# Three depthwise-conv tiles as half-length filters that are summed by accumulating transfers

## The chip, the cores and the metric

The kernel runs on one core of a Trainium2 chip, in one launch. The time is device microseconds for the whole program, median of 3 runs. TensorE is called PE here, VectorE DVE, ScalarE ACT, GpSimd POOL and SyncE SP, as in the profile. All data is float32. A matmul of float32 operands is done as three matmuls in a shorter format: each operand is split into a rounded part (`hi`) and the remainder (`lo`), and hi*hi, hi*lo and lo*hi are summed in PSUM. So every weight tile and every activation tile needs a cast (on ACT) and a subtraction that gives the remainder.

## What is computed

One layer over 1024 tokens and 1024 channels:

```python
h = rmsnorm(x, norm_g) * (1 + scale(c)) + shift(c)
cv, cg, cs, lx, ls = split(h @ w_in)              # 5 x 1024 columns
v = cv * sigmoid(cg)
v = causal_depthwise_conv(v, dw_w, dw_b)          # 31 taps for each channel
v = silu(layernorm(v, cln_g, cln_b))              # over channels
y_conv = (v @ pw2_w + pw2_b) * silu(cs)
xs = causal_depthwise_conv(lx, sc_w, sc_b)        # 4 taps
r, i = sigmoid(xs @ wr + br), sigmoid(xs @ wi + bi)   # 8 blocks of 128
y_lru = linear_scan(a(r), bx(r, i, xs)) * silu(ls)
x = rmsnorm(x + (1 + gate(c)) * (concat(y_conv, y_lru) @ w_out), final_g)
```

## The kernel before, in words

Channels lie on the 128 partitions, tokens along the free dimension, so an activation is eight tiles of 128 x 1024 float32 (512 KB). A weight tile of 128 output channels is also 128 x 1024. PE works through slots: a slot is one output tile, 8 contraction steps x 3 products x 2 halves of the tokens, 48 matmuls of 128 x 512 (`mm_k`, L432 to 450). The slots' order stands in `slots` (L377 to 392): first the tiles for conv tiles 0 and 1, then the tiles of the recurrence, mixed with those for conv tiles 2 to 7; then eight slots (`lru`) that multiply the recurrence's output with its half of `w_out`. After the layer norm of the conv result come the pointwise projection (`papw`, `pbpw`) and the rest of `w_out` (`paout`, `pbout`, `out`).

Each engine works in order through its own queue. The order is not written by hand: `Plan` (L83 to 245) takes every operation with an engine, a cost, a priority and what it reads and writes, plays the kernel through with these costs, and emits the operations in the order in which they started there. What the chip then does later than the plan, the queues' order doesn't follow. The plan holds DVE operations with operands in SBUF and POOL operations apart from each other (`lock`). Tiles come from pools: 47 tiles of 128 x 1024 in SBUF (`big`), in PSUM three tiles of 128 x 1024 for matmuls (`mm`) and one for accumulation (`acc`).

What the change touches:

- `weights` and `w_slice` (L410 to 430): load a weight tile (SP), cast to `whi` (ACT), remainder `wlo` by a subtraction `SUB` (L323), on POOL except for the four `out` tiles at the end.
- `gate_mod` (L1028) and `dot` (L710): eight dot products of a row of `mod_w` with the conditioning vector: on POOL a multiply, then on ACT a sum along the row; on DVE one operation.
- `gw_load` (L949): remainders of the gate weights, on POOL.
- `conv_tile` (L886 to 938): the 31 taps. For the tiles in `POOLED`, 2 and 5, ACT makes a product `cq` of the shifted tile with each tap, 30 of them at full length, and POOL adds each to the tile (`c<-c,cq`). For the other six the tokens are parted into even and odd, and three filters of half length run on DVE: one over the even tokens, one over the odd ones, one over their sums with taps summed in pairs. Each tap is one multiply-add of up to 512 elements into the accumulator `cacc` in PSUM; the two outputs are then put together. Conv work has the lowest priority (1000 and up), behind all that PE waits for.
- `conv_sum` (L940): the sum of the eight conv tiles, on POOL but for the last; `layer_norm` (L1037): the mean by PE from it, then mean, variance and their broadcast.
- `evac_in` (L961): takes a finished tile out of PSUM; the multiply that gives `v` reads pairs of tokens (`by_two`) and writes even and odd ones apart (`apart`).

Of the kernel before, what the change touches and what calls it, by code (L numbers as in the profile page):

```python
# [45 lines left out]
POOLED = (2, 5)  # L46
# [6 lines left out]
SUMS = (0, 1, 3, 2, 4, 6, 5, 7)  # L53
QRES = 4
GM = 22
# [22 lines left out]
class Op:  # L78
    __slots__ = ("eng", "cost", "emit", "prio", "table", "bufs", "succ", "wait", "ready",
                 "seq", "reserve", "columns", "lock", "end", "psum")  # L80


class Plan:  # L83
# [7 lines left out]
    def __init__(self, pools):  # L91
        self.pools = pools
        self.ops, self.writer, self.readers = [], {}, {}
# [13 lines left out]
    def op(self, eng, cost, emit, prio, r=(), w=(), table=None, after=(), reserve=0,  # L107
           columns=0, lock=False):
        o = Op()
        o.eng, o.cost, o.emit, o.prio, o.table = eng, cost, emit, prio, table  # L110
# [28 lines left out]
    def order(self):  # L139
# [19 lines left out]
        def done(o, end):  # L159
            o.end = until[o.eng] = end  # L160
# [14 lines left out]
        while left:  # L175
# [3 lines left out]
            for e in engines:  # L179
# [42 lines left out]
                if e == "POOL" and held["DVE"] > t + 1e-9:  # L222
                    waiting, until[e] = o, float("inf")
                    continue
# [24 lines left out]
def hymba_layer(ctx: ExitStack, tc: tile.TileContext, xT, c_row, vecs, mod_w, w_first, w_in,  # L249
# [11 lines left out]
    psacc = ctx.enter_context(tc.tile_pool(name="psacc", bufs=1, space=bass.MemoryType.PSUM))  # L261
# [8 lines left out]
    pools["acc"] = (psacc, "acc", [P, T], 1)  # L270
# [46 lines left out]
    def TT(prio, eng, out, a, b, op, n=T, r=(), w=(), reserve=0, after=()):  # L317
        e = dve if eng == "DVE" else pool
        return S.op(eng, d_cost(n) if eng == "DVE" else p_cost(n),
                    lambda: e.tensor_tensor(out=out(), in0=a(), in1=b(), op=op), prio, r, w,  # L320
                    reserve=reserve, lock=not in_psum(r), after=after)

# [104 lines left out]
    def weights(s, after=(), n=None, eng="POOL"):  # L427
        n = number[s] if n is None else n
        w_bufs(s)
# [25 lines left out]
    def acc_tile(name, parts=2):  # L455
        return S.buf("acc", name, F32, parts)
# [187 lines left out]
    psf = [mm_tile(f"first{n}", 4) for n in range(3)] + [acc_tile("first3", 4)]  # L644
    psb = psf[3]
# [15 lines left out]
    def fw_mm(prio, ps, i, xh, xl, k, cols, after=()):  # L661
        _, wh, wl = fw[k - k % 2]

        def emit():
            for lhs, rhs, last in ((wh, xh, 0), (wh, xl, 0), (wl, xh, 1)):
                for a, b in cols:
                    pe.matmul(ps()[:, a:b], fw_part(lhs, k, i * P, i * P + P)(),  # L667
# [92 lines left out]
    st, wk = ctile("st", KT), halves(psb, H, T)  # L760

    def stats(sq, k):
        for b in range(KT):
            pe.matmul(psb()[:, H + b:H + b + 1], sq()[:, b * P:b * P + P], ones[:, 0:1],
                      start=k == 0 and b == 0, stop=k == len(sqs) - 1, skip_group_check=True)

    def spread_mm(a, e):
        for b in range(a // P, e // P):
            o = H + b * P - a
# [4 lines left out]
    ACT(RSP, lambda: st, lambda: psb()[:, H:H + KT], AF.Sqrt, KT, bias=eps_t, scale=1.0 / D,  # L774
        r=wk, w=[("st", 0)])
    S.op("DVE", 0.12, lambda: dve.reciprocal(st, st), RSP, [("st", 0)], [("st", 0)])
    for a, e in START:
        spread = S.op("PE", 0.22 * ((e - a) // P), lambda a=a, e=e: spread_mm(a, e), RSP,
                      [("st", 0)], wk, columns=4 * (e - a))
        ACT(RSP, part(rbc, a, e), part(psb, H, H + e - a), "copy", e - a, r=wk,  # L780
# [83 lines left out]
    def by_two(b, a, e):  # L864
        return lambda: b()[:, a:e].rearrange("p (m q) -> p m q", q=2)

    def apart(b, a, e):
        return lambda: b().rearrange("p (q m) -> p m q", q=2)[:, a // 2:e // 2]
# [16 lines left out]

    def conv_tile(i):  # L886
# [6 lines left out]
        if i in POOLED:  # L893
            ACT(pr, ci, vi, AF.Identity, scale=w(0), bias=vec("dw_b", i), r=[vi, ("V", 1)],
                w=[ci])
            for s in range(1, TAPS):
                q = big_buf(f"cq{i}_{s}")
                ACT(pr, part(q, s, T), part(vi, 0, T - s), AF.Copy, T - s, scale=w(s), r=[vi],
                    w=[q], reserve=QRES)
                TT(pr, "POOL", part(ci, s, T), part(ci, s, T), part(q, s, T), ALU.add, T - s,  # L900
                   r=[ci, q], w=[ci])
            c[i] = ci
            return


        acc, b2 = acc_tile(f"cacc{i}"), bias2[:, i:i + 1]
        acc_e, acc_s, src_s = half(acc, 0), half(acc, 1), half(ci, 0)
# [8 lines left out]
        def every(o):  # L916
            return lambda: ci().rearrange("p (m q) -> p q m", q=2)[:, o]
        TT(pr, "DVE", src_s, ev, od, ALU.add, H, r=[vi], w=[(ci, 0)])
        ACT(pr, acc_e, ev, AF.Identity, H, scale=w(0), bias=vec("dw_b", i), r=[vi, ("V", 1)],
            w=[(acc, 0)])  # L920
        ACT(pr, acc_s, src_s, AF.Identity, H, scale=ws(0), bias=b2,
            r=[(ci, 0), ("V", 1), ("wsum", 0)], w=[(acc, 1)])
        for r in range(1, 16):
            STT(pr, cut(acc_e, r, H), cut(ev, 0, H - r), w(2 * r), cut(acc_e, r, H), ALU.mult,
                ALU.add, H - r, r=[vi, (acc, 0)], w=[(acc, 0)])
            STT(pr, cut(acc_s, r, H), cut(src_s, 0, H - r), ws(r), cut(acc_s, r, H), ALU.mult,
                ALU.add, H - r, r=[(ci, 0), (acc, 1)], w=[(acc, 1)])
        ACT(pr, every(1), acc_s, "copy", H, r=[(acc, 1)], w=[ci])
        ACT(pr, acc_s, od, AF.Copy, H, scale=w(1), r=[vi], w=[(acc, 1)])
        for r in range(1, 15):  # L930
            STT(pr, cut(acc_s, r, H), cut(od, 0, H - r), w(2 * r + 1), cut(acc_s, r, H), ALU.mult,
                ALU.add, H - r, r=[vi, (acc, 1)], w=[(acc, 1)])
        ACT(pr, every(0), acc_e, "copy", H, r=[(acc, 0)], w=[ci])
        TT(pr, "DVE", every(1), every(1), acc_e, ALU.subtract, H, r=[ci, (acc, 0)], w=[ci])
        TT(pr, "DVE", every(1), every(1), acc_s, ALU.subtract, H, r=[ci, (acc, 1)], w=[ci])
        TT(pr, "DVE", cut(every(0), 1, H), cut(every(0), 1, H), cut(acc_s, 0, H - 1), ALU.add,
           H - 1, r=[ci, (acc, 1)], w=[ci])
# [11 lines left out]
    def gw_load(i, n):  # L949
# [4 lines left out]
        SUB(n - 3, "POOL", lo, r, hi, 2 * P, r=[r, hi], w=[lo])  # L954
# [6 lines left out]
    def evac_in(m, ps, n, b=None, rb=()):  # L961
# [5 lines left out]
        elif kind == CV:  # L967
            sg = sig.pop(i)
            if i in POOLED:
                v[i] = sg  # L970
                TT(pr, "DVE", sg, ps, sg, ALU.mult, r=[ps, sg], w=[sg])
            else:
                v[i] = big_buf(f"v{i}")
# [331 lines left out]
```

## Time and profile before

| | |
|---|---|
| median of 3 runs | 770.2 us (769.64 to 770.25) |
| the profiled execution | 771.28 us |
| its span, first to last instruction | 769.4 us |
| mean granted TensorE clock | 0.985 of full speed |
| shares of the chain that ended last | PE 57%, DVE 29%, ACT 7%, POOL 3% |

The profile is one execution on the chip. A row of a timeline gives start and duration in us, the engine, the line of the kernel (often that of a helper: L438 is every slot's matmul, L320 every tensor_tensor, L312 every scalar_tensor_tensor, L301 and L293 ACT's operations), what is written and read, how many in a row, and in brackets the idle time ahead of it and the operation that ended it. A row of groups gives, after the bar, busy us, mean ns of one, and idle time. A row of stretches gives for each engine its busy time and in brackets the number of operations, then the granted clock, the busy share of the 16 DMA engines and GB/s. Matmuls overlap, so that one takes longer than the distance to the next.

### The profile page before, as it was taken

How to read it: one execution, taken by the hardware profiler on the slowest of the kernel's cores; microseconds unless marked ns; L12 is line 12 of the kernel's file. 1: busy time of each engine (PE TensorE's matmuls, PEld its weight loads, DVE VectorE, ACT ScalarE, POOL GpSimd, SP SyncE). 2: the span in 40 equal slices, each digit the busy share in tenths (PEclk: the TensorE clock that was granted, in tenths of full speed). 3: DMA queues.
4: the chain of work that ended last, by engine and by line, in shares of the span. 5: the costliest groups of instructions: out<-in, count | busy, mean ns of one | idle time of the engine just before them, and what ended most of it. 6: DMA issues, size and time to landing. Idle time of an engine off the chain costs nothing.

```text
span 769.4 us, 8629 instructions
## 1 busy us (share of the span) xinstructions
PE 733.5 (95%) x3288; PEld 606.0 (79%) x3288; DVE 665.6 (87%) x806; ACT 420.3 (55%) x473; POOL 323.1 (42%) x132
## 2 busy tenths in 40 slices
PE   3999899999999997999999998999999999999995
PEld 2888677888888885888888787788888888887885
DVE  7999999789899889999897998995977666999565
ACT  6630926997626477955956565664723223455220
POOL 0030312799899469989999612121220000000000
PEclk9999999999999999899999999999999999999997
DMA  9930221102102312331111012433332621425114
GB/s 329 406 118 32 83 82 35 55 27 83 63 28 83 116 55 83 116 110 56 55 55 55 27 55 81 138 136 111 136 115 96 200 110 40 152 83 177 43 55 164
DMA packets 24954, 77.84 MB, mean 101 GB/s; under 512 B 2768, under 2 KB 6096, under 8 KB 24912
## 3 DMA queue, kind: packets, MB, share of 16 engines
q1 hardware_dynamic: 24912, 77.28, 28.5%
q8 instruction: 26, 0.43, 0.2%
q14 instruction: 16, 0.13, 0.1%
HBM read 64.68 MB, written 12.58 MB: 100 GB/s over the span
## 4 chain that ended last, share of the span: by engine, by line
PE 57%; DVE 29%; ACT 7%; POOL 3%; issue 2%; DMA 1%; SPq 0%; DVEq 0%; ACTq 0%; POOLq 0%
PE ps L438 32%; DVE cacc L312 11%; PE first L667 6%; PE papw L559 5%; PE pbpw L559 4%; PE out L605 3%; ACT cq L301 3%; PE paout L559 2%; DVE r L1020 2%; PE pbout L559 2%; DVE xs L312 1%; DVE xs L320 1%; DVE yl L320 1%; DVE sls L320 1%; POOL c L320 1%
## 5 line engine op out<-in xcount | busy, mean ns | idle before, releaser
L320 POOL TENSOR_TENSOR wlo<-raw,whi 128x1024 fp32r<-128x1024 f32 x44 | 115.1, 2615 | 234.5 <-ACT whi L293 234.5
L438 PE MATMUL ps<-uh,whi 128*128 128x512 f32 x576 | 180.5, 395 | 7.0 <-ACT scs L301 6.6
L438 PE MATMUL ps<-ul,whi 128*128 128x512 f32 x576 | 179.7, 393 | 3.6 <-DVE ul L312 3.6
L438 PE MATMUL ps<-uh,wlo 128*128 128x512 f32 x576 | 179.3, 393 | 1.6 <-POOL wlo L320 1.6
L320 POOL TENSOR_TENSOR c<-c,cq 128x1023 f32<-128x1023 f32 (+29 forms) x60 | 159.8, 2663 | 9.5 <-ACT cq L301 7.0
L312 DVE SCALAR_TENSOR_TENSOR cacc<-v,V,cacc 128x511 f32<-128x511 f32 (+14 forms) x174 | 129.6, 745 | 13.7 <-ACT c L293 6.3
L438 PEld LDWEIGHTS ps<-uh,whi 128*128 128x128 f32 x576 | 109.4, 191 | 31.4 <-ACT scs L301 7.5
L438 PEld LDWEIGHTS ps<-ul,whi 128*128 128x128 f32 x576 | 109.3, 190 | 27.7 <-DVE ul L312 4.7
L438 PEld LDWEIGHTS ps<-uh,wlo 128*128 128x128 f32 x576 | 109.2, 190 | 24.8 <-POOL wlo L320 2.0
L293 ACT CAST whi<-raw 128x1024 fp32r<-128x1024 f32 x48 | 50.3, 1047 | 59.6 <-issue 34.4
L301 ACT ACTIVATE cq<-sig,V 128x1023 f32<-128x1023 f32 (+29 forms) x60 | 63.9, 1128 | 1.6 <-POOL c L320 1.6
L312 DVE SCALAR_TENSOR_TENSOR cacc<-c,wsum,cacc 128x511 f32<-128x511 f32 (+6 forms) x84 | 62.7, 746 | 2.3
L301 ACT ACT_TABLE_LOAD x45 | 57.7, 1283 | 1.6 <-PEq L1297 0.7
L438 PE MATMUL ps<-yh,whi 128*128 128x512 f32 x128 | 39.6, 391 | 0.0
L438 PE MATMUL ps<-yh,wlo 128*128 128x512 f32 x128 | 39.4, 389 | 0.0
L438 PE MATMUL ps<-yl,whi 128*128 128x512 f32 x128 | 39.4, 389 | 0.0
L667 PE MATMUL first<-uh,fhi 128*128 128x512 f32 x64 | 26.7, 416 | 11.1 <-ACT uh L301 11.1
L312 DVE SCALAR_TENSOR_TENSOR xs<-ps,V,xs 128x1023 f32<-128x1023 f32 (+2 forms) x24 | 30.6, 1274 | 2.6 <-ACT xs L301 2.5
L438 PEld LDWEIGHTS ps<-yl,whi 128*128 128x128 f32 x128 | 24.0, 188 | 5.0
L438 PEld LDWEIGHTS ps<-yh,wlo 128*128 128x128 f32 x128 | 24.0, 188 | 5.0
L667 PE MATMUL first<-ul,fhi 128*128 128x512 f32 x64 | 26.3, 411 | 1.7 <-DVE ul L312 1.7
L438 PEld LDWEIGHTS ps<-yh,whi 128*128 128x128 f32 x128 | 23.9, 188 | 4.9
(299 smaller groups left out, 1359.7 us busy)
## 6 DMA issues: line engine op xcount, KB each, us to landing
raw<-in_w_in_dram SPq DMA_DIRECT2D x36, 512.0 KB, 3.3
modw<-in_mod_w_dram SPq DMA_DIRECT2D x24, 512.0 KB, 7.8
raw<-in_w_out_dram SPq DMA_DIRECT2D x12, 512.0 KB, 3.9
scsd<-scs SPq DMA_DIRECT2D x8, 512.0 KB, 2.6
acc<-in_xT_dram SPq DMA_DIRECT2D x8, 512.0 KB, 4.6
accd<-acc SPq DMA_DIRECT2D x8, 512.0 KB, 2.8
rawpw<-in_pw_dram SPq DMA_DIRECT2D x8, 512.0 KB, 3.8
scsr<-scsd SPq DMA_DIRECT2D x8, 512.0 KB, 5.3
```

Source lines behind the costliest of these rows:

```text
L293: act.copy(out(), in_())
L301: act.activation(out=out(), in_=in_(), func=func, **kw)
L312: dve.scalar_tensor_tensor(out=out(), in0=in0(), scalar=scalar, in1=in1(), op0=op0, op1=op1, accum_out=accum)
L320: lambda: e.tensor_tensor(out=out(), in0=a(), in1=b(), op=op), prio, r, w,
L438: pe.matmul(ps()[:, a - off:b - off], k3(lhs)()[:, k, :], rhs[k]()[:, a:b], start=(k == 0 and lhs is wh and rhs is xh and (a - off) % H == 0),
L559: pe.matmul(half(*ps)(), half(*lhs)()[:, j * P:j * P + P], half(*rhs)(), start=start and j == 0 and z == 0, stop=j == KT // 2 - 1 and z == ...
L605: pe.matmul(ps()[:, a - off:e - off], k3(lhs)()[:, k, :], rhs()[:, i * H + a % H:i * H + a % H + e - a], start=k == KORD[0] and lhs is wh ...
L667: pe.matmul(ps()[:, a:b], fw_part(lhs, k, i * P, i * P + P)(), rhs()[:, a:b], start=k == 0 and lhs is wh and rhs is xh, stop=k == KT - 1 a ...
L1020: S.op("DVE", 2.2, lambda: dve.tensor_tensor_scan(out=r(), data0=a(), data1=xs(), initial=0.0, op0=ALU.mult, op1=ALU.add), pr, [a, xs], [r])
```

## The change

Tiles 2, 3 and 5 become `POOLED`, and `POOLED` now means something else. Such a tile is parted into even and odd tokens like the others, and its three filters run at half length, but each tap's product is made by ACT in SBUF, and the products are added by transfers that POOL issues and that accumulate in their destination. The products of the even filter and of the sum filter lie in one tile of two halves, so that one transfer adds both; the odd filter has its own transfers of half the length. Each transfer has one contiguous row for each partition. A product waits for the fourth last addition (`AHEAD`). Beside this:

- remainders of weight tiles from number 10 on (`EARLY`), of gate weights (`GLO`) and the gate dots (`GDOT`) go to DVE;
- the plan knows transfers with a cost of issue, a flight time and a rate (`ISSUE`, `FLIGHT`, `RATE`), without the lock between DVE and POOL;
- the accumulator becomes two tiles of half the length, each with its own filter; mean and its broadcast go to `mm` tiles; a conv tile waits until the one before has begun its second filter (`held`);
- `v` is written in another element order for all eight tiles; the order of `conv_sum` changes (`SUMS`).

```diff
-POOLED = (2, 5)
+POOLED = (2, 3, 5)
...
-SUMS = (0, 1, 3, 2, 4, 6, 5, 7)
+SUMS = (0, 1, 3, 2, 6, 4, 7, 5)
 QRES = 4
+AHEAD = 4
+PAD = 16
+GLO = "DVE"
+GDOT = "DVE"
+FOLD = "DVE"
+EARLY = 10
+ISSUE, FLIGHT, RATE = 1.0, 7.0, 3.0
...
-        o.lock = eng == "POOL" or eng == "DVE" and lock
+        o.lock = not lag and eng == "POOL" or eng == "DVE" and lock
...
-            o.end = until[o.eng] = end
+            until[o.eng] = end
+            if o.lag:
+                self.adder = max(self.adder + o.lag, end + FLIGHT)
+                end = self.adder
+            o.end = end
...
-    psacc = ctx.enter_context(tc.tile_pool(name="psacc", bufs=1, space=bass.MemoryType.PSUM))
+    psacc = ctx.enter_context(tc.tile_pool(name="psacc", bufs=2, space=bass.MemoryType.PSUM))
...
-    pools["acc"] = (psacc, "acc", [P, T], 1)
+    pools["acc"] = (psacc, "acc", [P, H], 2)
...
+    def ADD(prio, out, a, n=T, r=(), w=(), after=()):
+
+        return S.op("POOL", ISSUE, lambda: pool.dma_start(out(), a(), accum_op=ALU.add), prio, r,
+                    w, lag=RATE * n / T, after=after)
...
-    def weights(s, after=(), n=None, eng="POOL"):
+    def weights(s, after=(), n=None, eng=None):
         n = number[s] if n is None else n
+        eng = eng or ("POOL" if n < EARLY else "DVE")
...
     def by_two(b, a, e):
-        return lambda: b()[:, a:e].rearrange("p (m q) -> p m q", q=2)
+        return lambda: b()[:, a:e].rearrange("p (m q) -> p q m", q=2)
...
+        if i in POOLED:
+            S.op("POOL", 0.1, lambda: pool.memset(ci()[:, :PAD], 0.0), pr, [vi],
+                 [(ci, 0)])
+            TT(pr, "DVE", part(ci, PAD, PAD + H), ev, od, ALU.add, H, r=[vi], w=[(ci, 0)])
+            conv_pooled(i, pr, ci, vi, (ev, od), (w, ws), every)
+            return
...
+    def conv_pooled(i, pr, ci, vi, src, wts, every):
+
+
+        (ev, od), (w, ws) = src, wts
+        es, oo, adds = big_buf(f"es{i}", parts=2), big_buf(f"oo{i}"), []
+
+        def product(to, z, r, x, key, scale, bias=None):
+            ACT(pr, part(to, z * H + (0 if z else r), z * H + H), x,
+                AF.Copy if bias is None else AF.Identity, H - (0 if z else r), bias=bias,
+                scale=scale, r=[key, ("V", 1), ("wsum", 0)], w=[(to, z if to.parts > 1 else 0)],
+                after=adds[-AHEAD:][:len(adds) // AHEAD][:1])
+        for r in range(16):
+            q = es if r == 0 else big_buf(f"cq{i}_{r}", parts=2)
+            product(q, 0, r, lambda r=r: ev()[:, :H - r], vi, w(2 * r),
+                    None if r else vec("dw_b", i))
+            product(q, 1, r, part(ci, PAD - r, PAD - r + H), (ci, 0), ws(r),
+                    None if r else bias2[:, i:i + 1])
+            if r:
+                adds.append(ADD(pr, part(es, r, T), part(q, r, T), r=[es, q], w=[es]))
+            if r > 14:
+                continue
+            q = oo if r == 0 else big_buf(f"co{i}_{r}")
+            product(q, 0, r, lambda r=r: od()[:, :H - r], vi, w(2 * r + 1))
+            if r:
+                adds.append(ADD(pr, part(oo, r, H), part(q, r, H), H, r=[oo, q], w=[oo]))
+        ACT(pr, every(1), half(es, 1), "copy", H, r=[es], w=[ci])
+        ACT(pr, every(0), half(es, 0), "copy", H, r=[es], w=[ci])
+
+        def last(eng, o, a, e, src, off, op):
+            TT(pr, eng, lambda: every(o)()[:, a:e], lambda: every(o)()[:, a:e],
+               part(src, off, off + e - a), op, e - a, r=[ci, src], w=[ci])
+        last(FOLD, 1, 0, H, es, 0, ALU.subtract)
+        last(FOLD, 1, 0, H, oo, 0, ALU.subtract)
+        last(FOLD, 0, 1, H, oo, 0, ALU.add)
         c[i] = ci
...
-        SUB(n - 3, "POOL", lo, r, hi, 2 * P, r=[r, hi], w=[lo])
+        SUB(n - 3, GLO, lo, r, hi, 2 * P, r=[r, hi], w=[lo])
...
-        dot("POOL", n, 2 * KT + j)
+        dot(GDOT, n, 2 * KT + j)
...
-        mean = acc_tile("mean")
+        mean = mm_tile("mean")
...
-        bc = acc_tile("lnbc")
+        bc = mm_tile("lnbc")
```

More of the change, by code (lines that the diff above doesn't have):

```diff
@@ L221, in order @@
                         free[b.pool] -= 1
-                if e == "POOL" and held["DVE"] > t + 1e-9:
+                if e == "POOL" and o.lock and held["DVE"] > t + 1e-9:
                     waiting, until[e] = o, float("inf")
@@ L779, in hymba_layer @@
                       [("st", 0)], wk, columns=4 * (e - a))
-        ACT(RSP, part(rbc, a, e), part(psb, H, H + e - a), "copy", e - a, r=wk,
+        ACT(RSP, part(rbc, a, e), part(psb, 0, e - a), "copy", e - a, r=wk,
             w=halves(rbc, a, e))
@@ L884, in hymba_layer @@
     csum = big_buf("csum")
+    held = []
     def conv_tile(i):
@@ L892, in conv_tile @@
         ci, vi = big_buf(f"c{i}", parts=2), v[i]
[L893 to L907, printed above, removed]
+        b2, src_s = bias2[:, i:i + 1], half(ci, 0)
         ev, od = (lambda: vi()[:, :H]), (lambda: vi()[:, H:])
@@ L919, in conv_tile @@
+        acc_e, acc_s = half(acc, 0), half(acs, 0)
         ACT(pr, acc_e, ev, AF.Identity, H, scale=w(0), bias=vec("dw_b", i), r=[vi, ("V", 1)],
-            w=[(acc, 0)])
-        ACT(pr, acc_s, src_s, AF.Identity, H, scale=ws(0), bias=b2,
-            r=[(ci, 0), ("V", 1), ("wsum", 0)], w=[(acc, 1)])
+            w=[acc], after=held[-1:])
+        o = ACT(pr, acc_s, src_s, AF.Identity, H, scale=ws(0), bias=b2,
+            r=[(ci, 0), ("V", 1), ("wsum", 0)], w=[acs])
+        held.append(o)
         for r in range(1, 16):
```

67 lines of the change are left out of this document (34 added, 33 removed).

## The prediction, made before the changed kernel was run

> **What bounds the kernel now.** I read four views: the page's totals, busy time in stretches of 20 us, the timeline of TensorE (PE), and what ScalarE (ACT) and GpSimd (POOL) did ahead of each hole in it.
>
> ```profile
> span 769.4 us, 8629 instructions
> ...
> PE 733.5 (95%) x3288; PEld 606.0 (79%) x3288; DVE 665.6 (87%) x806; ACT 420.3 (55%) x473; POOL 323.1 (42%) x132
> ```
>
> PE is the bound: 36 us of the span are not covered by matmuls, and part of that is the head, before inputs arrive, and the tail. The change removes no matmul, so all it can win is holes in PE. Where they are:
>
> ```profile
> core 0: us, PE busy (x) PEld busy (x) DVE busy (x) ACT busy (x) POOL busy (x), PEclk, DMA share, GB/s
> 20.00:40.00 20.00, 20.00 (x99) 16.83 (x97) 20.00 (x34) 13.52 (x19) 0.00 (x0) 1.00 1.03 407
> 80.00:100.00 20.00, 16.42 (x72) 12.84 (x71) 20.00 (x24) 17.25 (x23) 7.63 (x2) 0.95 0.30 100
> 280.00:300.00 20.00, 18.42 (x82) 14.91 (x81) 16.97 (x21) 18.33 (x22) 20.00 (x9) 1.00 0.18 63
> 300.00:320.00 20.00, 15.81 (x60) 12.54 (x59) 17.77 (x22) 16.18 (x20) 19.84 (x9) 0.83 0.28 105
> 340.00:360.00 20.00, 20.00 (x90) 16.57 (x89) 19.47 (x23) 14.00 (x18) 17.80 (x8) 1.00 0.11 36
> 460.00:480.00 20.00, 17.59 (x71) 14.12 (x70) 17.54 (x20) 10.39 (x11) 4.99 (x2) 0.92 0.19 66
> 480.00:500.00 20.00, 19.91 (x86) 15.95 (x85) 19.75 (x20) 12.48 (x12) 2.88 (x2) 1.00 0.42 145
> ```
>
> An undisturbed stretch (340 to 360) holds 90 matmuls, 0.222 us each. Counting matmuls instead of busy time also catches the lower granted clock after a hole (0.83 at 300 to 320). Missing are 18 at 80 to 100 (4.0 us), 8 + 30 at 280 to 320 (**8.4 us**), and 19 + 4 at 460 to 500 (**5.1 us**). The holes themselves:
>
> ```profile
> 96.72 0.49 PE L438 MATMUL ps<-ul,whi 128*128 128x512 f32 x1 [3.41 <-DVE ul L312]
> 290.75 0.72 PE L438 MATMUL ps<-uh,wlo 128*128 128x512 f32 x2 [1.58 <-POOL wlo L320]
> 307.95 1.22 PE L438 MATMUL ps<-uh,whi 128*128 128x512 f32 x2 [4.19 <-ACT scs L301]
> 476.87 1.22 PE L438 MATMUL ps<-uh,whi 128*128 128x512 f32 x2 [2.41 <-ACT scs L301]
> ```
>
> The releaser of two of them is ACT's evacuation `scs`, 1 us of work; the question is why ACT was late.
>
> ```profile
> 295.40 3.38 POOL L320 TENSOR_TENSOR c<-c,cq 128x1021 f32<-128x1021 f32 x1
> 301.10 2.40 POOL L320 TENSOR_TENSOR modw<-modw,sc 128x1024 f32<-128x1024 f32 x1
> 303.53 1.06 ACT L301 ACTIVATE modw<-modw 128x1024 f32<-128x1024 f32 x1 [5.14 <-POOL modw L320]
> 306.88 1.01 ACT L301 ACTIVATE scs<-ps 128x1024 f32<-128x1024 f32 x1
> 473.93 0.61 ACT L293 COPY c<-cacc 128x512 f32<-128x512 f32 x1 [7.03 <-DVE cacc L312]
> ```
>
> At 280 to 320 POOL is full (20.00 and 19.84 of 20): tap additions of tile 5, weight remainders, gate dots and the channel sum queue behind each other. ACT, which works in order, stood 5.14 us before the gate dot's second half with `scs` behind it. At 470 it stood 7.03 us before a conv copy, because VectorE (DVE) was late with its taps. So one hole pair comes from a full POOL, the late one from a late DVE.
>
> DVE is late in part because POOL makes it wait:
>
> ```profile
> 138.28 9.09 POOL L320 TENSOR_TENSOR c<-c,cq 128x1023 f32<-128x1023 f32 x3 [4.61 <-ACT cq L301]
> 138.62 3.14 DVE L320 TENSOR_TENSOR sls<-sls,r 128x1024 f32<-128x1024 f32 x1
> 459.96 2.27 DVE L1020 TENSOR_TENSOR_SCAN r<-a,xs 128x1024 f32<-128x1024 f32 x1
> 495.65 1.21 DVE L320 TENSOR_TENSOR sls<-sls,r 128x1024 f32<-128x1024 f32 x1
> ...
> L1020 DVE TENSOR_TENSOR_SCAN r<-a,xs 128x1024 f32<-128x1024 f32 x8 | 27.6, 3453 | 0.0
> L320 DVE TENSOR_TENSOR sls<-sls,r 128x1024 f32<-128x1024 f32 x8 | 19.1, 2384 | 0.0
> L320 DVE TENSOR_TENSOR xs<-xs,r 128x1024 f32<-128x1024 f32 x8 | 17.1, 2143 | 0.0
> L320 DVE TENSOR_TENSOR yl<-sls,yh 128x1024 fp32r<-128x1024 f32 x8 | 13.8, 1729 | 0.8 <-ACT yh L293 0.7
> L320 DVE TENSOR_TENSOR c<-v 128x512 f32<-128x512 f32 x6 | 8.3, 1387 | 0.0
> L320 DVE TENSOR_TENSOR c<-c,cacc 128x512 f32<-128x512 f32 x12 | 8.3, 688 | 0.4
> ```
>
> The same multiply takes 1.21 us at 495, with POOL idle, and 3.14 us inside a POOL addition. Against 1.21 us (2.27 for the scan, 0.69 for half length) the five groups lose 9.4 + 9.5 + 7.5 + 4.2 + 4.2 = 35 us of DVE time.
>
> **The change part by part.**
>
> ```profile
> L312 DVE SCALAR_TENSOR_TENSOR cacc<-v,V,cacc 128x511 f32<-128x511 f32 (+14 forms) x174 | 129.6, 745 | 13.7 <-ACT c L293 6.3
> L312 DVE SCALAR_TENSOR_TENSOR cacc<-c,wsum,cacc 128x511 f32<-128x511 f32 (+6 forms) x84 | 62.7, 746 | 2.3
> L320 POOL TENSOR_TENSOR wlo<-raw,whi 128x1024 fp32r<-128x1024 f32 x44 | 115.1, 2615 | 234.5 <-ACT whi L293 234.5
> L312 DVE SCALAR_TENSOR_TENSOR modw<-modw,sc 128x1024 f32<-128x1024 f32 x16 | 21.6, 1358 | 1.9 <-DMA modw<-in_mod_w_dram 1.9
> L301 ACT ACTIVATE cq<-sig,V 128x1023 f32<-128x1023 f32 (+29 forms) x60 | 63.9, 1128 | 1.6 <-POOL c L320 1.6
> 474.57 0.69 ACT L301 ACTIVATE cacc<-v,V 128x512 f32<-128x512 f32 x1
> ```
>
> *DVE.* Tile 3 leaves: a sixth of 129.6 + 62.7, so -32. Of 44 weight remainders the six with numbers 4 to 9 stay on POOL; 38 come at 1.21: +46. Eight gate dots at 1.36: +11. Eight gate-weight remainders, a quarter of a full one: +2.5. Four half-length steps (prepare, fold) for tiles 2 and 5: 8 x 0.69 = +5.5. Port waits: up to -35, since about 12 of some 130 POOL operations remain. The sum is -2 us; up to the mean at 499 us, without the seven remainders after it, -10. DVE is not relieved by much, but its waits go.
>
> *POOL.* 60 additions (159.8 us on the page), 38 remainders and the dots leave; 87 transfer issues come. It is no longer a bound, and ACT no longer waits for its dot: the second half (8 x 1.24 us on ACT) goes too.
>
> *ACT.* 60 full products (63.9 us) become 3 x 47 half-length ones at 0.69: 97 us. With the dots gone, tile 3's own steps gone and six copies added it ends near 440 us, 57% of the span. This hides behind PE as long as nothing in ACT's order waits long.
>
> *The transfers* are the unknown: no row of before shows an accumulating transfer. Each tile has a chain of 15 full additions (512 KB), each of which needs the one before it, and beside it 14 half ones. The nearest rows are plain:
>
> ```profile
> scsd<-scs SPq DMA_DIRECT2D x8, 512.0 KB, 2.6
> modw<-in_mod_w_dram SPq DMA_DIRECT2D x24, 512.0 KB, 7.8
> ```
>
> The low end for one link is 2.6 us. 512 KB at 407 GB/s take 1.29 us. Estimate: 2.6 + 1.29 for reading the sum as well + 1.29 for the half addition in flight (twice a half) + 1.2 for issue (a short POOL operation) = **6.4 us**. High end: 7.8 (loads queued behind each other) + 1.29 + 1.2 = 10.3. I take 6.4, since the DMA share is 0.1 to 0.4 in the conv stretch, nearer to the lone store. In bytes: 3 x (15 + 7) x 2.58 = 170 us of all 16 engines, spread over 136 to 499 us, on top of a share near 0.2: about 0.67, no bound.
>
> The Trainium skill ("Collectives: The Full Stack", Part 3, the bandwidth ceiling) says that an add in a transfer needs two source reads and so runs at half the rate of a copy. "DMA: Bandwidth & Descriptors" (Anatomy of one DMA) gives 2.0 us fixed plus bytes over 436 GB/s: by both an estimated 4.4 us plus issue. No run so far shows either; the sum goes by 6.4.
>
> What decides is the written-out order: it was laid out with 1.0 us issue and 7.0 us flight (the diff's ISSUE and FLIGHT), so **8.0 us a link**. Each product waits for the addition four earlier, in ACT's queue, and behind it stand weight casts, `sig`, `scs` and `xs`, for which PE waits. With links under 8.0 us every such wait is over when reached.
>
> ```profile
> 276.50 1.25 ACT L301 ACTIVATE c<-sig,V 128x1024 f32<-128x1024 f32 x1 [2.51 <-DVE sig L320]
> 499.18 1.98 PE mean L1043 x4
> ```
>
> The last filtered tile, 5, starts at 276.5; 15 links of 8.0 end it at 397, of 10.3 at 431. The mean does not wait for it.
>
> *Moved at no cost.* Mean and its broadcast take one of three matmul tiles instead of the accumulator: two remain, and an evacuation of 1.3 us fits into the 10.7 us (48 x 0.222) of a slot; without this cover, 1.3 us a slot. The accumulator in two halves lets the next tile begin earlier. The other element order of `v` can move eight operations either way by half their length, 5 us of DVE, none of PE. The start (4.0 us) stays: its two remainders stay on POOL.
>
> *Sum.* The holes at 280 to 320 (8.4) and 460 to 500 (5.1) go. For one new wait I book 1.6, the shortest hole above. 771.28 - 11.9 = 759.4 for the profiled execution, which stands 1.1 over the median of 770.2: **758.3 us**.
>
> **The rivals.**
>
> *Links longer than planned* (slower). ACT then slips against its order at each product and PE with it, once the 10.7 us of a finished slot are used up. Tiles 2 and 3 run side by side, 5 later: about 30 links in a row. At 9.0 us: 30 x 1.0 - 11 = +19, so 777; at 10.3: 30 x 2.3 - 11 = +58, so 816. It decides from 8.0 + 11/30 = 8.4 us. For it: loads that land in 7.8 us in a crowd. Against it: conv stretches are not crowded. Chance 0.25.
>
> *DVE becomes late instead of POOL* (same or a little faster). It now makes PE's remainders in order and was at 17 to 20 of 20. Only the POOL pair goes: 758.3 + 5.1 = 763; with new holes as large as the old, 770. Chance 0.17.
>
> *Descriptors held up by DVE.* If a transfer's issue must wait for a running DVE operation, a link grows by 1.21, or 2.27 beside a scan: 7.6 to 8.7 us, at most 30 x 0.7 - 11 = +10, so 758 to 768. The Trainium skill ("SBUF — State Buffer", the "DVE blocks DMA" trap) describes this for two-port DVE modes and says elsewhere there that an operation with two SBUF inputs only hinders GpSimd's reads; by that it should not occur here. The trace shows only compute against compute. Chance 0.06.
>
> **How the numbers follow.** The forecast has 0.52; by itself 752.5 (the start hole goes as well, nothing new) to 764. About 0.2% is what a measurement of this kernel can tell from no change: below 768.7 is faster, above 771.7 slower. Faster: 0.52 + 0.11 of the DVE case + 0.03 = 0.66. Same: 0.07. Slower: 0.25 + 0.02 = 0.27. The range is 752.5 to 788: it takes in the DVE and descriptor cases and links up to 9.4 us (30 x 1.4 - 11 = 31), leaving out the rest of the long links.
>
> **What would show it.** Right: 90 matmuls in each stretch from 120 to 500 us; `sls` and scan near 1.21 and 2.27 us; POOL almost empty; full additions landing in under 7 us. Wrong: ACT waiting for transfers or for buffers that transfers read, granted clock under 1 in the conv stretches, PE released by `whi` or `sig` after such a wait; or, for the DVE case, PE released by DVE's `wlo`.

## The result, and the profile after

The changed kernel takes 764.42 us (median of five runs, 762.58 to 765.98), the kernel before 770.2 beside it: a ratio of 0.9926 [0.9904, 0.9948], faster by 5.8 us. The forecast was 758.3, faster by 11.9. The time lies inside the range and the sign was right, but half of the gain did not come. The profiled execution took 763.61 us, 7.7 less than the one before.

The totals of the page after, the busy share of the DMA engines in 40 slices, and two queues (packets, MB, share of 16 engines; q0 is POOL's, with the additions):

```profile
span 761.7 us, 8802 instructions
...
PE 729.1 (96%) x3288; PEld 603.5 (79%) x3288; DVE 631.0 (83%) x832; ACT 434.9 (57%) x537; POOL 111.0 (15%) x108
...
DMA  9930221598999999897971012342332531325114
...
q1 hardware_dynamic: 24912, 77.28, 28.7%
q0 software_dynamic: 12528, 34.26, 25.1%
```

POOL is nearly empty as meant (111 us where it was busy for 323), ACT is where it was put (435 against some 440), and DVE lost 35 us. New is the run of nines (and a few sevens and eights) in the DMA row: the DMA engines are all but full from the 9th slice to the 21st, 152 to 400 us.

The groups of DVE that answer to those of before (busy us, mean ns of one, idle before):

```profile
L1069 DVE TENSOR_TENSOR_SCAN r<-a,xs 128x1024 f32<-128x1024 f32 x8 | 18.3, 2284 | 0.1
L332 DVE TENSOR_TENSOR sls<-sls,r 128x1024 f32<-128x1024 f32 x8 | 9.7, 1217 | 0.0
L332 DVE TENSOR_TENSOR wlo<-raw,whi 128x1024 fp32r<-128x1024 f32 x42 | 53.3, 1268 | 6.9 <-ACT whi L305 6.9
L332 DVE TENSOR_TENSOR v<-ps,sig 128x1024 f32<-128x1024 f32 x6 | 7.3, 1222 | 3.0 <-PE ps L456 2.9
```

Scan and `sls` take 2.28 and 1.22 us each instead of 3.45 and 2.38: the waits beside POOL's additions are gone from them. Stretches of PE after (columns as before the change; the two long ones were chosen for the DMA share):

```profile
core 0: us, PE busy (x) PEld busy (x) DVE busy (x) ACT busy (x) POOL busy (x), PEclk, DMA share, GB/s
160.00:180.00 20.00, 20.00 (x90) 16.57 (x89) 19.86 (x26) 15.71 (x21) 5.46 (x7) 1.00 0.91 185
280.00:300.00 20.00, 19.69 (x87) 15.96 (x86) 11.96 (x15) 10.65 (x15) 6.85 (x8) 1.00 1.08 234
300.00:320.00 20.00, 15.09 (x59) 12.36 (x60) 6.42 (x7) 16.51 (x22) 2.67 (x4) 0.91 0.93 245
420.00:440.00 20.00, 18.66 (x82) 14.71 (x81) 20.00 (x23) 9.70 (x10) 0.00 (x0) 1.00 0.15 52
460.00:480.00 20.00, 20.00 (x90) 16.57 (x89) 16.75 (x21) 12.34 (x12) 2.94 (x1) 1.00 0.37 132
160.00:340.00 180.00, 174.79 (x765) 144.29 (x764) 136.45 (x168) 139.75 (x184) 57.01 (x65) 0.99 0.99 216
140.00:400.00 260.00, 254.79 (x1117) 210.62 (x1116) 212.72 (x261) 197.04 (x258) 81.40 (x90) 0.99 0.93 202
```

The late loss (460 to 480) is gone: 90 matmuls. At 420 to 440 a new one cost 8 matmuls, 1.8 us. And at 280 to 320 still 3 + 31 matmuls are missing, 34 x 0.222 = 7.5 us where 8.4 stood before. At 300 to 320 DVE and POOL are mostly idle (6.42 and 2.67 of 20), where they were nearly full before (17.77 and 19.84). The hole is in the old place and has another cause. The holes themselves:

```profile
96.53 0.63 PE L456 MATMUL ps<-ul,whi 128*128 128x512 f32 x1 [1.79 <-DVE ul L324]
304.91 1.20 PE L456 MATMUL ps<-uh,whi 128*128 128x512 f32 x2 [5.21 <-ACT scs L313]
436.28 0.73 PE L1057 MATMUL gate<-xsl,ghi 128*128 128x512 f32 x2 [0.99 <-DVE xsl L332]
```

PE is released by ACT's `scs`, as before. What ACT did ahead of it:

```profile
282.46 0.72 ACT L313 ACTIVATE cq<-v,V 128x509 f32<-128x509 f32 x1 [0.89 <-DMA oo<-co]
287.20 1.05 ACT L305 CAST xsh<-xs 128x1024 fp32r<-128x1024 f32 x1 [3.40 <-DMA es<-cq]
290.87 0.72 ACT L313 ACTIVATE co<-v,V 128x509 f32<-128x509 f32 x1 [2.62 <-DMA oo<-co]
294.84 1.28 ACT L313 ACT_TABLE_LOAD   x1 [2.13 <-DMA oo<-co]
297.47 0.72 ACT L313 ACTIVATE cq<-v,V 128x500 f32<-128x500 f32 x1 [0.31 <-DMA es<-cq]
301.68 0.71 ACT L313 ACTIVATE cq<-v,V 128x499 f32<-128x499 f32 x1 [0.78 <-DMA es<-cq]
303.84 1.01 ACT L313 ACTIVATE scs<-ps 128x1024 f32<-128x1024 f32 x1
```

In some 22 us ACT stood 0.89 + 3.40 + 2.62 + 2.13 + 0.31 + 0.78 = 10.1 us for additions that had not landed, and `scs`, which reads no transfer's data, stood behind them. The cast `xsh` and the table load ahead of `sls` belong to the recurrence and read nothing that an addition writes either: by the program, what makes them wait is that their output takes over the place of a tile that an addition still reads. Additions landed late:

```profile
es<-cq POOLq DMA_DIRECT2D x3, 511.0 KB, 10.2
es<-cq POOLq DMA_DIRECT2D x3, 509.5 KB, 5.0
es<-cq POOLq DMA_DIRECT2D x3, 505.0 KB, 8.1
```

The medians of the 15 groups of full additions lie between 5.0 and 10.2 us.

### The profile page after: what moved, and what is told of

It is laid out like the page before. It is cut to its first block, busy times and chain, and to the rows that moved or that the text cites. A ratio compares the mean times of both kernels' runs of the same rounds, so it can differ in the third digit from the quotient of the medians.

```text
span 761.7 us, 8802 instructions
## 1 busy us (share of the span) xinstructions
PE 729.1 (96%) x3288; PEld 603.5 (79%) x3288; DVE 631.0 (83%) x832; ACT 434.9 (57%) x537; POOL 111.0 (15%) x108
## 3 DMA queue, kind: packets, MB, share of 16 engines
q1 hardware_dynamic: 24912, 77.28, 28.7%
q0 software_dynamic: 12528, 34.26, 25.1%
## 4 chain that ended last, share of the span: by engine, by line
PE 57%; DVE 21%; DMA 9%; issue 9%; POOL 2%; ACT 2%; SPq 0%; DVEq 0%; POOLq 0%; ACTq 0%
PE ps L456 32%; DMA es<-cq 8%; PE first L685 5%; PE papw L577 5%; PE pbpw L577 4%; DVE caccs L324 3%; PE out L623 3%; PE paout L577 3%; PE pbout L577 2%; DVE cacc L324 2%; DVE wlo L332 2%; DVE x L324 1%; DVE xs L324 1%; DVE ul L324 1%; DMA modw<-in_mod_w_dram 1%
## 5 line engine op out<-in xcount | busy, mean ns | idle before, releaser
L332 DVE TENSOR_TENSOR wlo<-raw,whi 128x1024 fp32r<-128x1024 f32 x42 | 53.3, 1268 | 6.9 <-ACT whi L305 6.9
L324 DVE SCALAR_TENSOR_TENSOR cacc<-v,V,cacc 128x511 f32<-128x511 f32 (+14 forms) x75 | 55.5, 740 | 0.0
L337 POOL DMA_DIRECT2D es<-cq x45 | 40.1, 896 | 94.1 <-ACT cq L313 44.2
L324 DVE SCALAR_TENSOR_TENSOR caccs<-v,V,caccs 128x511 f32<-128x511 f32 (+6 forms) x70 | 52.1, 745 | 1.0
L324 DVE SCALAR_TENSOR_TENSOR caccs<-c,wsum,caccs 128x511 f32<-128x511 f32 (+6 forms) x70 | 51.9, 741 | 0.4
L337 POOL DMA_DIRECT2D oo<-co x42 | 37.6, 920 | 93.3 <-ACT co L313 38.3
L324 DVE SCALAR_TENSOR_TENSOR modw<-modw,sc 128x1024 f32<-128x1024 f32 x24 | 31.4, 1313 | 12.2 <-DMA modw<-in_mod_w_dram 12.2
L685 PE MATMUL first<-uh,fhi 128*128 128x512 f32 x56 | 23.3, 416 | 11.1 <-ACT uh L313 11.1
L313 ACT ACTIVATE cq<-v,V 128x511 f32<-128x511 f32 (+14 forms) x45 | 31.8, 709 | 3.4 <-DMA es<-cq 2.5
L332 POOL TENSOR_TENSOR wlo<-raw,whi 128x1024 fp32r<-128x1024 f32 x6 | 18.3, 3061 | 97.6 <-ACT whi L305 97.6
```

Source lines behind the costliest of these rows:

```text
L313: act.activation(out=out(), in_=in_(), func=func, **kw)
L324: dve.scalar_tensor_tensor(out=out(), in0=in0(), scalar=scalar, in1=in1(), op0=op0, op1=op1, accum_out=accum)
L337: return S.op("POOL", ISSUE, lambda: pool.dma_start(out(), a(), accum_op=ALU.add), prio, r, w, lag=RATE * n / T, after=after)
L685: pe.matmul(ps()[:, a - off:b - off], fw_part(lhs, k, i * P, i * P + P)(), rhs()[:, a:b], start=k == 0 and lhs is wh and rhs is xh, stop=k ...
```

## The experiments

**Theory**: the DMA engines are full while three tiles are summed; additions land later than the plan's 8.0 us, and what waits in ACT's queue for data or for a place opens PE's hole at 305. **Rivals**: ACT has too much to do there; POOL's issues are held up by DVE; the gain that remains is the remainders leaving POOL, or the element order of `v`, and the transfers bring nothing. All ran in five rounds beside the kernel before (770.1 to 770.8). Ratios are against that kernel.

**Short additions.** In the changed kernel each addition moves the first 64 of its elements; the order of all queues stays.

```diff
-        return S.op("POOL", ISSUE, lambda: pool.dma_start(out(), a(), accum_op=ALU.add), prio, r,
+        return S.op("POOL", ISSUE, lambda: pool.dma_start(out()[:, :64], a()[:, :64], accum_op=ALU.add), prio, r,
```

> The changed kernel with the same order on every engine and the same 87 accumulating transfers, but each moves only the first 64 elements of its row (256 bytes a row instead of up to 4 KB): most of each addition is left out. Theory (the 16 DMA engines are full between 160 and 340 us, share 0.91 to 1.08, so transfers land later than the order assumes, and ACT stands before buffers that a transfer still reads; PE's 5.21 us hole at 305 us is its consequence): full additions land in 2 to 5 us instead of 5 to 10, ACT's waits for transfers between 283 and 302 us (about 11 us) vanish, the hole at 305 us shrinks to under 1.5 us, and 31 + 3 missing matmuls there (7.6 us) come back: 764.4 - 6 = 756 to 760 us. Rival (what costs is the number of dependent links, their issue on POOL at 0.9 us each and the order itself, not the bytes): hole of 4 us or more stays, 763 to 766 us.

Measured 754.52 us, 0.9785 [0.976, 0.9811]. Landings (median us, last column), and the stretch of 180 us:

```profile
es<-cq POOLq DMA_DIRECT2D x45, 32.0 KB, 2.5
oo<-co POOLq DMA_DIRECT2D x42, 32.0 KB, 2.3
```

```profile
160.00:340.00 180.00, 180.00 (x796) 149.10 (x795) 145.50 (x180) 146.03 (x195) 59.48 (x67) 1.00 0.39 94
```

796 matmuls instead of 765, and no wait of ACT for an addition; the time is below the 756 to 760 us that I expected. As many issues, products and waits are there, and as many packets (12528); only most of the bytes are gone, 2.86 MB of 34.26 being left. So neither ACT's work nor POOL's issues make the hole; the bytes do. The spans differ by 761.7 - 752.5 = 9.2 us.

**A plan with a slower transfer.** The changed kernel, with only the plan's figures changed: flight 8.0 us, 4.0 us between two full additions.

```diff
-ISSUE, FLIGHT, RATE = 1.0, 7.0, 3.0
+ISSUE, FLIGHT, RATE = 1.0, 8.0, 4.0
```

> The changed kernel with the same work, but laid out with a slower transfer: flight 8.0 us instead of 7.0 and 4.0 us instead of 3.0 for a full addition after another. Theory (full DMA engines, so the order's 3.0 us is too short: 191 us of all engines for 66 full additions is 2.9 us each with nothing else running, and plain loads take a quarter of the engines): ACT's waits before buffers get shorter because the order gives buffers back later; the hole at 305 us shrinks by half or more, 759 to 763 us. Rival (the order's numbers do not matter, because ACT in order waits for the same transfers wherever the products stand, or DVE then becomes late): 764 to 768 us.

Measured 757.47 us, 0.9821 [0.9794, 0.9847]. The same stretch, and the hole that is left behind it:

```profile
160.00:340.00 180.00, 180.00 (x795) 149.10 (x795) 139.46 (x170) 132.10 (x171) 50.35 (x57) 1.00 0.90 199
```

```profile
475.07 1.96 PE L1092 MATMUL mean<-csum,ones_d 128*128 128x512 f32 x4 [1.66 <-DVE csum L332]
```

The time is below the 759 to 763 us that I expected. The DMA engines are still 0.90 busy, and the additions land hardly sooner (medians of 4.6 to 8.9 us), yet PE is full. Engines that are nearly full don't by themselves cost PE anything; an order that expects the results too early does.

**Remainders and dots alone.** The kernel before, with weight remainders from number 10 on, gate-weight remainders and gate dots on DVE; POOL keeps its additions.

```diff
-    def weights(s, after=(), n=None, eng="POOL"):
+    def weights(s, after=(), n=None, eng=None):
         n = number[s] if n is None else n
+        eng = eng or ("POOL" if n < 10 else "DVE")
...
-        SUB(n - 3, "POOL", lo, r, hi, 2 * P, r=[r, hi], w=[lo])
+        SUB(n - 3, "DVE", lo, r, hi, 2 * P, r=[r, hi], w=[lo])
...
-        dot("POOL", n, 2 * KT + j)
+        dot("DVE", n, 2 * KT + j)
```

> The kernel before, with one part of the change alone: remainders of weight tiles from number 10 on, of gate weights, and the gate dots on DVE; tiles 2 and 5 are still added by POOL, tile 3 stays on DVE, no accumulating transfers. Theory of the prediction (the holes at 290 and 308 us of the kernel before come from a full POOL, behind whose dot ACT stands): both holes vanish, 8.4 us come back; but DVE, with 46 + 11 + 2.5 us more and tile 3 still its own, gets late and gives back 5 to 15 us around 440 to 500 us: 768 to 778 us. Rival (DVE has room, and moving the remainders is most of the gain): 760 to 765 us.

Measured 796.99 us, 1.0332 [1.0306, 1.0358]: far worse than any theory had it. DVE is busy for 720 us, and PE waits from 210 us on. The three longest waits before 400 us, and DVE's remainders:

```profile
225.78 0.73 PE L439 MATMUL ps<-uh,wlo 128*128 128x512 f32 x2 [2.62 <-DVE wlo L320]
316.59 1.22 PE L439 MATMUL ps<-uh,whi 128*128 128x512 f32 x2 [6.01 <-ACT scs L301]
356.43 0.80 PE L439 MATMUL ps<-uh,wlo 128*128 128x512 f32 x2 [4.10 <-DVE wlo L320]
...
L320 DVE TENSOR_TENSOR wlo<-raw,whi 128x1024 fp32r<-128x1024 f32 x42 | 65.8, 1568 | 0.2 <-ACT whi L293 0.2
```

So the remainders gain nothing by themselves: DVE has no room for them as long as it filters six tiles and POOL's additions hold it up (a remainder takes 1.57 us here, 1.27 in the changed kernel).

**The channel sum on DVE**, in the changed kernel, against the new hole at 436, ahead of which DVE and POOL held each other up:

```profile
408.06 3.26 POOL L332 TENSOR_TENSOR csum<-csum,c 128x1024 f32<-128x1024 f32 x1
408.99 3.41 DVE L332 TENSOR_TENSOR wlo<-raw,whi 128x1024 fp32r<-128x1024 f32 x1
433.44 1.05 ACT L305 CAST xsh<-xs 128x1024 fp32r<-128x1024 f32 x1 [10.23 <-DVE xs L324]
```

```diff
-            a, eng = (c[SUMS[0]] if i == SUMS[1] else csum), "DVE" if i == SUMS[-1] else "POOL"
+            a, eng = (c[SUMS[0]] if i == SUMS[1] else csum), "DVE"
```

> The changed kernel with the six additions of the channel sum on DVE instead of POOL. Theory (the new hole at 436 us, 1.34 us of PE, comes from DVE being 2.2 us late, because a remainder that takes 1.21 us took 3.41 us at 409 us beside a POOL addition of the channel sum): no DVE operation above its undisturbed time there, hole gone, 1 to 2 us faster than the changed kernel, 762 to 764 us. Rival (six additions of 1.21 us are as much DVE time as the waits that they cause, so nothing is won): 764 to 766 us.

Measured 763.14 us (761.0 to 765.17), 0.9893 [0.9864, 0.9923]. The hole at 436 is replaced by one of 1.02 us at 412; the one at 305 stays with 5.54. The 1.3 us below the changed kernel lie within the spread of the two (762.58 to 765.98 there).

**The element order of `v` alone**, in the kernel before:

```diff
-        return lambda: b()[:, a:e].rearrange("p (m q) -> p m q", q=2)
+        return lambda: b()[:, a:e].rearrange("p (m q) -> p q m", q=2)
...
-        return lambda: b().rearrange("p (q m) -> p m q", q=2)[:, a // 2:e // 2]
+        return lambda: b().rearrange("p (q m) -> p q m", q=2)[:, :, a // 2:e // 2]
```

> The kernel before with one part of the change alone: the multiply that gives v takes its elements in the other order (all even ones, then all odd ones); the order on every engine is unchanged. Theory (the start of the changed kernel gained some 2 us because this multiply is shorter: 1278 instead of 1686 ns at half length, 1222 instead of 2044 ns at full length in the two profiles): both durations fall here too, although GpSimd adds as before, the hole at 96 us shrinks from 3.41 us to about 2, and the time falls by 1 to 3 us: 768 to 769.5. Rival (those durations were waits for GpSimd's port, so the order changes nothing): within 1 us of the kernel before.

Measured 766.49 us, 0.9944 [0.9921, 0.9966]: 4.3 us below the kernel before, more than the 1 to 3 that I expected, by eight operations:

```profile
L320 DVE TENSOR_TENSOR v<-ps,sig 128x1024 f32<-128x1024 f32 x4 | 4.9, 1214 | 0.0
L312 DVE SCALAR_TENSOR_TENSOR v<-first_u,bias,first_u 128x512 f32<-128x512 f32 x4 | 5.0, 1279 | 0.0
```

Before they took 2044 and 1686 ns each: 4 x 0.83 + 4 x 0.41 = 5.0 us of DVE.

**Plan figures and channel sum together** (both edits above):

```diff
-ISSUE, FLIGHT, RATE = 1.0, 7.0, 3.0
+ISSUE, FLIGHT, RATE = 1.0, 8.0, 4.0
...
-            a, eng = (c[SUMS[0]] if i == SUMS[1] else csum), "DVE" if i == SUMS[-1] else "POOL"
+            a, eng = (c[SUMS[0]] if i == SUMS[1] else csum), "DVE"
```

> The kernel with the slower transfer in the layout (flight 8.0, 4.0 us a full addition, 757.5 us) and the channel sum's additions on DVE as well. Theory (the port waits beside those additions are what is left late in the conv stretch): 755 to 757 us. Rival (what is left there is gone already with the other layout): 757 to 759 us.

Measured 754.23 us, 0.9767 [0.9734, 0.9799]. No hole of PE over 0.7 us is left between 100 and 660 us.

**A plan that is slower still.**

```diff
-ISSUE, FLIGHT, RATE = 1.0, 7.0, 3.0
+ISSUE, FLIGHT, RATE = 1.0, 9.0, 5.0
```

> The same layout change, further: flight 9.0 us and 5.0 us for a full addition. Theory (4.0 us is the rate that the chip gives, 2.9 us of full engines over the three quarters that plain loads leave; ACT still stood about 7 us in all before transfers at 4.0): the rest of the waits goes, PE's only holes are start and tail, 756 to 758 us, no more to win because PE is full there. Rival (a layout slower than the chip moves tile 5's end so late that the mean waits): 759 to 765 us. Second rival (the gain of the first layout change was a lucky order and not the rate): 762 us or more.

Measured 769.68 us, 0.9965 [0.9941, 0.9988]. I had expected 756 to 758 us. The conv stretch has no holes and ACT waits for no addition, as the theory has it. But POOL issues the last addition at 500 us instead of 391, PE begins the mean at 529 instead of 480, and behind the layer norm, where DVE is then busy without a gap (560 to 600 us), PE waits for it. That is the first rival, at a higher price than its 765. The time by itself would fit the second rival as well, but with no hole in the conv stretch the gain at 8.0 and 4.0 is not a lucky order:

```profile
583.64 0.80 PE L577 MATMUL papw<-vha,wlopw 128*128 128x512 f32 x1 [5.82 <-DVE wlopw L332]
592.47 0.80 PE L577 MATMUL papw<-vha,l34pw 128*128 128x512 f32 x1 [3.34 <-DVE l34pw L332]
```

**Two tiles by transfer instead of three**, first with the plan's 8.0 and 4.0, then with the change's own 7.0 and 3.0:

```diff
-POOLED = (2, 3, 5)
+POOLED = (2, 5)
...
-ISSUE, FLIGHT, RATE = 1.0, 7.0, 3.0
+ISSUE, FLIGHT, RATE = 1.0, 8.0, 4.0
```

> The layout with 8.0 and 4.0, but only tiles 2 and 5 by transfers; tile 3 is filtered on DVE as before. Theory (the third tile pays for the remainders that go to DVE: 32 us of DVE time against 59 us that come; without it DVE is late as it was in the kernel before with remainders alone, which took 797 us, less its 30 us of port waits): 768 to 785 us, PE released by DVE's wlo or by ACT behind DVE. Rival (without port waits DVE has room for three quarters of the load, and fewer transfers keep the DMA engines below full): 755 to 760 us.

Measured 754.12 us, 0.9768 [0.9736, 0.98]. I had held that DVE needs the third tile off it; it doesn't: with 658 us busy (88%) it still comes in time.

```diff
-POOLED = (2, 3, 5)
+POOLED = (2, 5)
```

> The changed kernel with only tiles 2 and 5 by transfers, laid out with the change's own numbers (flight 7.0, 3.0 us a full addition). Theory (the third tile is what fills the DMA engines; with two tiles their share is about 0.66 between 160 and 340 us and transfers keep to 3.0 us): ACT does not stand before transfers for more than 3 us in all, no hole at 305 us, 753 to 757 us as with the slower layout. Rival (transfers of 5 to 10 us from issue to landing come late whatever the load, so the layout's 7.0 and 3.0 are wrong in themselves): the hole near 305 us stays, 760 to 765 us.

Measured 755.96 us, 0.9799 [0.9764, 0.9834].

```profile
160.00:340.00 180.00, 180.00 (x796) 149.07 (x795) 168.35 (x210) 119.44 (x149) 38.49 (x39) 1.00 0.66 154
```

Unlike the change itself, it has no hole at 305 with the same plan figures (the longest is 1.13 us at 404, behind ACT's `sls`), and ACT waits for no addition. With the third tile the DMA engines are 0.99 busy, without it 0.66. The full additions land in 4.5 to 6.5 us (medians), so the rival, additions that are late at any load, falls.

**No tile by transfer**: all eight on DVE.

```diff
-POOLED = (2, 3, 5)
+POOLED = ()
```

> The changed kernel with no tile by transfers: all eight filtered on DVE, remainders and dots on DVE, GpSimd with six remainders and the channel sum. Theory (transfers pay, since DVE would be at 658 + 2 x 30 = 718 us of work, as in the 797 us kernel, which had 720): DVE late, PE holes behind wlo and scs, 775 to 800 us. Rival (what hurt the 797 us kernel were waits for GpSimd's port, 30 us and more, and the layout that knows them badly; without them DVE's 718 us still fit beside PE): 756 to 765 us.

Measured 796.43 us, 1.0319 [1.0279, 1.0358]. DVE is busy for 714 us, late at the layer norm, and PE's clock falls in the gaps:

```profile
603.06 0.79 PE L577 MATMUL papw<-vha,whipw 128*128 128x512 f32 x1 [11.02 <-ACT vha L305]
```

```profile
580.00:600.00 20.00, 7.32 (x32) 6.97 (x32) 16.13 (x18) 11.59 (x11) 0.00 (x0) 0.59 0.36 131
```

So the transfers do pay: two tiles of them are worth 796.4 - 756.0 = 40 us in this order of things, the third, with the change's figures, takes 8 of them back (764.4).

**Two tiles, the plan's 8.0 and 4.0, and the channel sum on DVE:**

```diff
-POOLED = (2, 3, 5)
+POOLED = (2, 5)
...
-ISSUE, FLIGHT, RATE = 1.0, 7.0, 3.0
+ISSUE, FLIGHT, RATE = 1.0, 8.0, 4.0
...
-            a, eng = (c[SUMS[0]] if i == SUMS[1] else csum), "DVE" if i == SUMS[-1] else "POOL"
+            a, eng = (c[SUMS[0]] if i == SUMS[1] else csum), "DVE"
```

> Two tiles by transfers, flight 8.0 and 4.0 us, and the channel sum on DVE: the two improvements on the three-tile layout together. Theory (with no hole between 120 and 660 us in either, PE is full and nothing is left to add): 752 to 756 us, no different from 754.1. Rival (both gains add, 3 us each below 757.5): 750 to 752 us.

Measured 753.69 us (752.74 to 755.53), 0.9775 [0.9741, 0.9809]. That is no different from 754.12 and 754.23: the three versions without a hole of PE over 0.9 us between 100 and 660 us end alike, some 16 us under the kernel before.

**The changed kernel with the old element order of `v`** (the edit of the `v` experiment undone):

```diff
-        return lambda: b()[:, a:e].rearrange("p (m q) -> p q m", q=2)
+        return lambda: b()[:, a:e].rearrange("p (m q) -> p m q", q=2)
...
-        return lambda: b().rearrange("p (q m) -> p q m", q=2)[:, :, a // 2:e // 2]
+        return lambda: b().rearrange("p (q m) -> p m q", q=2)[:, a // 2:e // 2]
```

> The changed kernel with one part undone: v written in the element order of the kernel before; ACT, PE and GpSimd keep their order. Theory (the order of v is worth 4.3 us by itself in the kernel before, and as much here): 767 to 770 us, start hole near 96 us back at 3 us or more, v at 1.1 to 1.3 us per half again only where it was. Rival (without GpSimd's additions the old order costs nothing, since its longer times were port waits): 763 to 766 us.

Measured 769.43 us, 0.9973 [0.9951, 0.9995].

```profile
96.42 0.50 PE L456 MATMUL ps<-ul,whi 128*128 128x512 f32 x1 [2.27 <-DVE ul L324]
307.40 1.22 PE L456 MATMUL ps<-uh,whi 128*128 128x512 f32 x2 [5.45 <-ACT scs L313]
```

By the medians the element order gives 5.0 of the change's 5.8 us, and all the rest of it together 0.8; by the ratios to the kernel before (0.9926 and 0.9973) it is 3.6 and 2.1. Either way most of the gain is the element order. The hole at the start is 2.27 us, not back at the 3 that I expected.

The lead over the kernel before, in matmuls begun by a given time (0.222 us each), from stretches of the profiled executions that start at 0:

| kernel | by 120 us | by 320 | by 440 | by 660 |
|---|---|---|---|---|
| the change | 9 | 16 | 8 | 30 |
| the change, old order of `v` | 4 | 2 | -5 | 15 |
| before, new order of `v` | 17 | 27 | 22 | 25 |
| short additions | 18 | 57 | 50 | 73 |
| the change, plan 8.0 and 4.0 | 14 | 52 | 50 | 64 |
| two tiles, plan 7.0 and 3.0 | 10 | 48 | 42 | 65 |

Row by row it says where time was won: the change with the old order of `v` is all but level with the kernel before at 320 us, so what it won by emptying POOL it lost to its transfers. The kernels whose additions were in time are 32 to 41 matmuls ahead of the change at that point.

## Why the prediction was right and wrong

*The hole at 280 to 320 goes, 8.4 us: wrong.* The reading of before was right, and its cause went: POOL is nearly empty, and ACT waits for no gate dot. But what was late next I had put at 1.6 us, and it was 7.5. The step that failed is the DMA share, "about 0.67, no bound". Its bytes were sized well: 25.1% of 761.7 us are 191 us of all 16 engines, against 170 forecast. Wrong was "spread over 136 to 499 us". In the trace POOL issues the first addition at 133 us and the last at 391. 191 us in some 260, and 0.2 below, give 0.93, the measured share from 140 to 400; from 160 to 340 it is 0.99. My own text had the last link end at 397, so the window could have been had from it: 170 us in 261, and 0.2 below, are 0.85.

*"With links under 8.0 us every such wait is over when reached": wrong.* The estimate of 6.4 us was near the middle: in the trace the 45 full additions take 6.5 us in the median from issue to landing. But 13 of them take over 8.0, up to 11.7, and the order waits for the late ones. With two tiles the median is 4.9 us, and one of 30 takes over 8.0. And I sought the wait only in the products. Two of the longer waits, 3.40 and 2.13 us, belong to operations outside the conv that take over a tile's place. Short additions, slower plan figures and a tile fewer each take the hole away; it is the mechanism of the first rival, which I gave 0.25. It was milder than its price, 19 us and more, since it hit one place; between 320 and 400 us ACT still waits for transfers, up to 5.70 us, and PE loses nothing:

```profile
340.93 1.21 ACT L305 COPY c<-es 128x512 f32<-128x512 f32 x2 [5.70 <-DMA es<-cq]
```

The plan's 3.0 us between additions is about what one takes from engines that do nothing else (191 us over 66 full ones are 2.9); it leaves no room for the loads beside them. That this is why 4.0 works is argued, not shown.

*The loss at 460 to 500, 5.1 us: mostly right.* It is gone; 1.8 us came back at 420 to 440. The experiment with the channel sum takes that hole away, but its time lies within the spread, so the price of the hole stays open.

*"5 us of DVE, none of PE": wrong.* The 5 us were right; PE got most of them, 4.3 in the kernel before and 3.6 to 5.0 in the changed one. I had the holes at 97 us (3.41 before DVE's `ul`) and knew DVE to be 20.00 of 20 busy there, and yet put operations on that stretch down as free. With it goes "the start stays": the hole at 97 shrank from 3.41 to 1.79 us. With the old order it is 2.27, so a part of that comes from the rest of the change; no run shows which. By the table, 5 of the 15 matmuls between the first two rows are won by 120 us, 9 more by 320.

*DVE, -2 us: wrong in size, without effect.* It was -34.6. Tile 3 (-33), remainders (+48) and dots (+10) came as put; by remainder, the waits beside POOL's operations ("port waits") were some 25 us more than I counted in five groups, which no view shows one by one, and `v` gave 6.6 (2039 to 1222 ns six times and 1704 to 1278 four times). It was not needed: with two tiles DVE is busy for 25 us more (656.1) and the kernel is faster.

*The DVE rival* came true in small: the hole at 436 is released by DVE's `xsl`, behind a cast that waited 10.23 us for DVE's `xs`. *The descriptor rival* is not seen: POOL's transfers are on its queue for 0.9 us each in the mean, and the short additions, with as many packets and DVE as busy, land in 2.3 to 2.5 us:

```profile
L337 POOL DMA_DIRECT2D es<-cq x45 | 40.1, 896 | 94.1 <-ACT cq L313 44.2
L337 POOL DMA_DIRECT2D oo<-co x42 | 37.6, 920 | 93.3 <-ACT co L313 38.3
```

By the table the profiled gain is 2.0 us (start) + 1.6 (to 320) - 1.8 (to 440) + 4.9 (to 660) + 1.0 (after it) = 7.7. So the sum missed by two errors of opposite sign: some 7.5 us at 300 that did not go, and gains from `v` that were not foreseen. That the time came out clearly below the kernel before is in the main luck: without the part that the forecast put at nothing for PE, the change is at 0.9973 [0.9951, 0.9995]. With two tiles, whose share of 0.66 is about what I had forecast for three, the time is 756.0, and even that has the help of `v`, which the forecast left out; two tiles without it were not run. Two bounds of the range were summed loosely: links of 9.4 us give 758.3 + 31 = 789, not 788, and 758.3 - 4.0 - 1.6 is 752.7, not 752.5; nothing hangs on either.

## What to carry to other kernels

When work is moved to transfers, spread their bytes over the window in which the order has them, not over the time in which the engine they relieve was busy; and look for waits not only where the data are read, but wherever a place in memory is taken over from a tile that a transfer still reads. When an order is laid out from estimated costs, a cost that is too low makes holes and one that is too high makes the end late: 7.0 and 3.0, 8.0 and 4.0, 9.0 and 5.0 gave 764, 757 and 770 us. A typical time is not enough for such a cost; the late ones decide. An operation that costs DVE half a microsecond is not free where the profile shows DVE full and PE waiting for it.

## What the runs showed of the hardware

An accumulating transfer from SBUF to SBUF took about twice the engine time of the plain ones beside it for the same bytes: 34.26 MB in 191 us of all engines are 179 GB/s, the plain queue's 77.28 MB in 28.7% of the span, 219 us, are 353. That agrees with the Trainium skill ("Collectives: The Full Stack", Part 3, the bandwidth ceiling), by which an add runs at half the rate of a copy. Additions of 32 KB landed in 2.3 to 2.5 us (DMA share 0.39), full ones (512 KB) in 4.5 to 6.5 with two tiles (0.66) and in 5.0 to 10.2 with three (0.99), all medians.

A DVE operation whose innermost dimension is a pair of elements, written half a tile apart, ran longer than the same elements in two long rows, read with a stride of two: 2.04 against 1.21 us for a multiply of 1024 elements, 1.10 against 0.74 for one of 512 with a scalar added (the last of its four in each profile). 1.21 us is also what the multiply `sls`, with plain rows throughout, takes (1.22), so the stride of two in reading cost nothing here. Whether the pairs cost through the short dimension or through the distance at which they are written is not shown.
